# Two gate pairs in seven quarter products in every feed-forward of a two-layer trunk, and the S5 preparation moved behind them

## Chip, core and metric

One core of a Trainium2 chip runs the whole program in one launch. The metric is the device time of one execution in microseconds (us), as the median of the runs shown.

## What is computed

Two layers, each a gated feed-forward, a token mixer and another gated feed-forward, on 256 tokens of 1024 columns; a norm at the end. The feed-forward is what the change touches:

```python
def swiglu(h, wg, wu, wd):
    return (jax.nn.silu(h @ wg) * (h @ wu)) @ wd      # wg, wu: 1024 x 2816, wd: 2816 x 1024

for l in range(2):
    x = x + 0.5 * swiglu(rmsnorm(x, ffn1_norm[l]), ffn1_wg[l], ffn1_wu[l], ffn1_wd[l])   # "a0", "a1"
    x = x + hybrid_mixer(rmsnorm(x, mix_norm[l]), ...)   # an S5 branch and an mLSTM branch
    x = x + 0.5 * swiglu(rmsnorm(x, ffn2_norm[l]), ffn2_wg[l], ffn2_wu[l], ffn2_wd[l])   # "b0", "b1"
return rmsnorm(x, final_norm)
```

The S5 branch needs tables that come from its parameters alone (exponentials, sines, small complex products), so they can be made ahead of it.

## The kernel before

**Split products.** All operands are float32. Each is split into a high and a low part, and every product takes three matmuls (`mm3`, L281 to L283: high x high, high x low, low x high). A weight tile of 128 x 1024 is loaded by a DMA on SP's queue (L239), ACT casts it to the high part `wh` (L263), and DVE subtracts that for the low part `wl` (L264). Six such pairs fit (`W_SLOTS`), and four raw tiles.

**A feed-forward** (`ffn`) goes over the 2816 columns in blocks of 512: b = 0 to 4, and a half block b = 5. A block is a gate `unit` (wg), a Silu on ACT, an up `unit` (wu), and a multiply on DVE (L580) that gives the hidden values `sg`. One block later `turns` transposes them on PE (L513, into PSUM tiles `hT`), and they are split again: ACT casts `hh` (L331), DVE subtracts for `hl` (L332). Then `project` multiplies with wd over 22 chunks k and adds to x. PSUM has four `mm` tiles for these sums and four `aux` tiles, which `hT` and the three tiles `qx`, `qy`, `qz` of a pair share.

**A pair** (`pair`, `seven`) does the gate products of two neighbouring blocks at once. Tokens, the 1024 inputs and the 1024 columns are each cut in two, and seven products of quarters stand for eight, as in Strassen's method in Winograd's form. A product is 12 matmuls of 512 columns. The sums of x's quarters are made once per feed-forward by `combine` (four DVE operations, L415 to L418, and four splits into `sh`, `sl`). The quarters of the weights are eight tiles `r` of 128 x 1024 (two each of `r00`, `r10`, `r01`, `r11`, in ten slots, loaded by L445). Sums of weight quarters replace the tiles in place: two by accumulating DMAs on POOL's queue (L452, `r00 += w01` after product 1, `r01 += w11`), two by DVE (L454). Each product's two tiles are cast on ACT (L459) and subtracted on DVE (`wl`, L460). Between the products stand the chunks of the two up units (`steps`, eight of them; multiply at L545), and `turns` comes at the second of eight steps. The products run in the order 1, 2, 5, 6, 7, 4, 3; `qy` holds product 2 until DVE adds it to `q1` (L476), `qz` holds product 5 until L490. In names, `wl_51_b0g3` is the second tile of product 5 in the pair that begins at block 3 of `b0`.

Before, `PAIRS` names one pair in the feed-forwards b: blocks 1 and 2 of `b0` and `b1`. All other blocks are plain.

**The S5 preparation** (`s5_prep`) is a generator of 19 steps, given to the feed-forwards a as `bg`. The order of the code is a request: a scheduler arranges the instructions on each engine as tiles and slots allow. `next(bg, None)` runs one step at each half of a plain block and at each k of `project`; `pair` calls it nowhere. With no pair in a feed-forward a, 12 steps stand in the blocks and the rest in `project`.

Of the kernel before, what the change touches and what calls it, by code (L numbers as in the profile page):

```python
# [35 lines left out]
B_SLOTS = 10  # L36
T_SLOTS = 8
N_S = 64
PAIRS = {"b": (1,)}
RS_SCALE = -(0.5**13)  # L40
NPAIR = 16
NC2 = L // 2
# [105 lines left out]
class Trunk:  # L148
# [351 lines left out]
    def ffn(self, normed, wg, wu, wd, name, after, bg=iter(())):  # L500
        nc = self.nc
        xh, xl = normed.out
        hT = []

        def turn(b, n, h):
            m = n // P
            new = self.a4 if b else self.v4
            hp = new([P, 4, L], f"hh_{name}_{b}", F32R)
            lp = new([P, 4, L], f"hl_{name}_{b}", F32R)
            for t in range(NT):  # L510
                pt = self.aux(f"hT_{name}_{b}_{t}").rearrange("p (a n) -> p a n", a=4)
                for a in range(m):
                    nc.tensor.transpose(pt[:, a, :], h[t][:, a * P : (a + 1) * P], self.ident)  # L513
                s = slice(t * P, (t + 1) * P)
                self.split(hp[:, :m, s], lp[:, :m, s], pt[:, :m, :])
            hT.extend((hp[:, a, :], lp[:, a, :]) for a in range(m))

        todo = []

        def turns():  # L520
            for i in todo:
                turn(*i)
            todo.clear()

        def pair(b, c0):

            sg = {}
            gate = self.seven(wg, c0, (xh, xl), sums, f"{name}g{b}")
            ups = [self.steps(wu, c0 + 512 * j, 512, xh, xl, f"{name}u{b + j}") for j in range(2)]
            for i in range(8):  # L530
                done = next(gate, {})
                for (t, j), g in done.items():
                    s = g if (t, j) != (1, 0) else self.t2([P, 512], f"sg_{name}_{b}_{t}")
                    nc.scalar.activation(s, g, AF.Silu, scale=normed.rs[t])
                    sg[t, j] = s
                if i == 1:
                    turns()
                ua = next(ups[i // 4])
                if i in (5, 7):
                    j = i // 6  # L540
                    if j == 0:
                        ua = first
                    for t in range(NT):
                        s = sg[t, j]
                        nc.vector.scalar_tensor_tensor(s, ua[t], normed.rs[t], s, op0=ALU.mult, op1=ALU.mult)  # L545
                    todo.append((b + j, 512, [sg[t, j] for t in range(NT)]))
                if i == 3:
                    first = ua

        pairs = PAIRS.get(name[0], ())  # L550
        sums = None
        for b, c0 in enumerate(range(0, DFF, 512)):
            if b in pairs:
                pair(b, c0)
            if b in pairs or b - 1 in pairs:
                continue
            n = min(512, DFF - c0)
            cold = normed.rs[0] is None
            with ExitStack() as order:
                if cold:  # L560
                    order.enter_context(self.behind())
                    order.enter_context(normed.first(0))
                ga = self.unit(wg, c0, n, xh, xl, f"{name}g{b}", (lambda: normed.turn(1)) if b == 0 else None,
                               early=[self.b4] * 4 if b == 0 else [], back=1 if cold else 2)
            if cold:
                with normed.first():
                    normed.whole()
            turns()
            sg = []
            with normed.first() if b == 0 else nullcontext():  # L570
                for t in range(NT):
                    s = self.t2([P, 512], f"sg_{name}_{b}_{t}")[:, :n]
                    nc.scalar.activation(s, ga[t], AF.Silu, scale=normed.rs[t])
                    sg.append(s)
                next(bg, None)
                ua = self.unit(wu, c0, n, xh, xl, f"{name}u{b}")
            if b == 0 and pairs:
                sums = self.combine(normed.quads, name)
            for t in range(NT):
                nc.vector.scalar_tensor_tensor(sg[t], ua[t], normed.rs[t], sg[t], op0=ALU.mult, op1=ALU.mult)  # L580
            next(bg, None)
            todo.append((b, n, sg))
        turns()
        return self.project(hT, wd, 0.5, name, W_SLOTS, after, bg)
# [738 lines left out]
```

## Time and profile before

| | |
|---|---|
| runs | 1238.13, 1237.85, 1237.78 us; median 1237.85 |
| profiled execution | 1238.24 us, its span 1236.5 us |
| PE / DVE / ACT / POOL busy | 99% / 74% / 58% / 2% of the span |
| instructions on PE / DVE / ACT | 6875 / 1594 / 1046 |
| DMA | 226.33 MB, mean 183 GB/s |
| granted TensorE clock | 0.999 |

PE is the tensor engine, DVE the vector engine, ACT the scalar engine, POOL the engine whose queue carries the accumulating DMAs. Busy is the share of time in which an engine runs an instruction; matmuls overlap in the trace, so the distance from one start to the next (the pitch) tells what one costs. `x12` behind a row is the number of such instructions. A bracket behind a row is idle time of that engine just before it and what ended it. In the program, `a0` runs from about 20 to 199 us, and blocks 1 to 4 of `b0` from about 457 to 549 us.

### The profile page before, as it was taken

What the parts mean: (1) busy time and instruction counts of PE and PEld (TensorE: products, weight loads), DVE (VectorE), ACT (ScalarE), POOL (GpSimd) and SP (SyncE); (2) the same over time, 40 slices, a digit from 0 to 9 for tenths busy, and PEclk for the clock granted to TensorE, in tenths of its full rate; (3) what the DMA queues carried; (4) which work ended last, traced back from release to release, by engine and by line L of the source; (5) the groups of instructions that cost most, each with busy time, mean ns of one, the idle gap of its engine ahead of it and who ended that gap; (6) DMA issues with size and microseconds to landing.
All of it is one profiled execution on the core that took longest, in us unless ns stands there. A gap on an engine that the chain in (4) does not pass through costs nothing.

```text
span 1236.5 us, 18416 instructions
## 1 busy us (share of the span) xinstructions
PE 1223.4 (99%) x6875; PEld 1052.9 (85%) x6875; DVE 912.2 (74%) x1594; ACT 716.2 (58%) x1046; POOL 26.5 (2%) x58
## 2 busy tenths in 40 slices
PE   9999999999999999999999999999999999999997
PEld 7888888989898888888888888889898978888886
DVE  7865856898989789654577668478989887885544
ACT  6455644655986467453455556365568854764441
POOL 2000000000000010000000000000000000100000
PEclk9999999999999999999999999999999999999999
DMA  7775574675555676665656655646645555956561
GB/s 242 237 195 178 143 226 122 195 217 148 165 169 171 209 222 182 204 185 178 200 172 190 191 177 165 202 144 196 203 137 154 174 167 187 288 173 186 173 210 44
DMA packets 130122, 226.33 MB, mean 183 GB/s; under 512 B 18328, under 2 KB 57456, under 8 KB 130032
## 3 DMA queue, kind: packets, MB, share of 16 engines
q1 hardware_dynamic: 127440, 219.88, 57.9%
q0 software_dynamic: 2528, 5.25, 2.1%
q8 instruction: 54, 0.88, 0.3%
q14 instruction: 36, 0.29, 0.1%
q10 hardware_dynamic: 64, 0.02, 0.0%
HBM read 223.01 MB, written 1.06 MB: 181 GB/s over the span
## 4 chain that ended last, share of the span: by engine, by line
PE 94%; DVE 3%; issue 2%; ACT 1%; DMA 0%; DVEq 0%; ACTq 0%
PE dn_b L282 3%; PE dn_b L281 3%; PE dn_b L283 3%; PE dn_a L281 3%; PE dn_a L282 3%; PE dn_a L283 3%; PE acc_a1g L281 2%; PE acc_a0g L282 2%; PE acc_a1g L283 2%; PE acc_a0u L281 2%; PE acc_b0u L281 2%; PE acc_a1u L282 2%; PE acc_b1u L281 2%; PE acc_a1u L283 2%; PE acc_b1u L283 2%; PE acc_a0u L283 2%
## 5 line engine op out<-in xcount | busy, mean ns | idle before, releaser
L264 DVE TENSOR_TENSOR wl_b<-raw_b,wh_b 128x1024 fp32r<-128x1024 f32 x44 | 53.9, 1225 | 60.9 <-ACT wh_b L263 60.9
L263 ACT CAST wh_b<-raw_b 128x1024 fp32r<-128x1024 f32 x44 | 46.3, 1052 | 68.1 <-PE dn_b L283 51.4
L264 DVE TENSOR_TENSOR wl_a<-raw_a,wh_a 128x1024 fp32r<-128x1024 f32 x44 | 53.6, 1221 | 34.9 <-ACT wh_a L263 34.9
L263 ACT CAST wh_a<-raw_a 128x1024 fp32r<-128x1024 f32 x44 | 45.9, 1050 | 44.2 <-PE dn_a L283 27.7
L281 PE MATMUL dn_a<-wh_a,hh_a 128*128 128x512 f32 x176 | 69.2, 393 | 0.0
L281 PE MATMUL dn_b<-wh_b,hh_b 128*128 128x512 f32 x176 | 69.0, 392 | 0.0
L282 PE MATMUL dn_a<-wl_a,hh_a 128*128 128x512 f32 x176 | 68.8, 391 | 0.0
L282 PE MATMUL dn_b<-wl_b,hh_b 128*128 128x512 f32 x176 | 68.8, 391 | 0.0
L283 PE MATMUL dn_b<-wh_b,hl_b 128*128 128x512 f32 x176 | 68.7, 390 | 0.0
L283 PE MATMUL dn_a<-wh_a,hl_a 128*128 128x512 f32 x176 | 68.5, 389 | 0.0
L283 PE MATMUL acc_g<-wh_g,xl_m 128*128 128x412 f32 (+1 forms) x160 | 56.7, 354 | 0.2
L281 PE MATMUL acc_g<-wh_g,xh_m 128*128 128x412 f32 (+1 forms) x160 | 56.4, 352 | 0.0
L282 PE MATMUL acc_g<-wl_g,xh_m 128*128 128x412 f32 (+1 forms) x160 | 55.9, 350 | 0.0
L263 ACT CAST wh_g<-raw_g 128x824 fp32r<-128x824 f32 (+1 forms) x40 | 34.9, 882 | 31.2 <-PE acc_g L283 10.9
L264 DVE TENSOR_TENSOR wl_g<-raw_g,wh_g 128x824 fp32r<-128x824 f32 (+1 forms) x40 | 40.1, 1012 | 14.4 <-ACT wh_g L263 14.1
L281 PEld LDWEIGHTS dn_a<-wh_a,hh_a 128*128 128x128 f32 x176 | 33.0, 188 | 7.1
L281 PEld LDWEIGHTS dn_b<-wh_b,hh_b 128*128 128x128 f32 x176 | 33.0, 188 | 7.1
L283 PEld LDWEIGHTS dn_a<-wh_a,hl_a 128*128 128x128 f32 x176 | 33.1, 188 | 7.0
L283 PEld LDWEIGHTS dn_b<-wh_b,hl_b 128*128 128x128 f32 x176 | 33.1, 188 | 6.9
L282 PEld LDWEIGHTS dn_b<-wl_b,hh_b 128*128 128x128 f32 x176 | 33.1, 188 | 6.9
L282 PEld LDWEIGHTS dn_a<-wl_a,hh_a 128*128 128x128 f32 x176 | 33.1, 188 | 6.7
L264 DVE TENSOR_TENSOR wl_a1g<-raw_a1g,wh_a1g 128x1024 fp32r<-128x1024 f32 x22 | 26.8, 1222 | 15.9 <-ACT wh_a1g L263 15.8
(593 smaller groups left out, 4020.1 us busy)
## 6 DMA issues: line engine op xcount, KB each, us to landing
raw_a<-in_ffn_wd_dram SPq DMA_DIRECT2D x44, 512.0 KB, 3.8
raw_b<-in_ffn_wd_dram SPq DMA_DIRECT2D x44, 512.0 KB, 3.6
raw_g<-in_w_in_dram SPq DMA_DIRECT2D x32, 412.0 KB, 4.2
raw_a0u<-in_ffn_wu_dram SPq DMA_DIRECT2D x22, 512.0 KB, 5.1
raw_b0u<-in_ffn_wu_dram SPq DMA_DIRECT2D x22, 512.0 KB, 4.5
raw_a1g<-in_ffn_wg_dram SPq DMA_DIRECT2D x22, 512.0 KB, 3.7
raw_a1u<-in_ffn_wu_dram SPq DMA_DIRECT2D x22, 512.0 KB, 4.0
raw_b1u<-in_ffn_wu_dram SPq DMA_DIRECT2D x22, 512.0 KB, 4.8
```

The lines of the kernel that those rows point to most:

```text
L263: nc.scalar.copy(wh[:, d], r[:, d])
L264: nc.vector.tensor_tensor(wl[:, d], r[:, d], wh[:, d].bitcast(F32), op=ALU.subtract)
L281: mm(ps, xh, wh, start=start, stop=False, skip_group_check=more)
L282: mm(ps, xh, wl, start=False, stop=False, skip_group_check=more)
L283: self.pe = mm(ps, xl, wh, start=False, stop=stop, skip_group_check=more).ins
```

## The change

`PAIRS` gets a second pair (blocks 3 and 4) in `b0` and `b1`, and both pairs in `a0` and `a1`: eight pairs instead of two. `combine` moves behind the multiply of block 0. Since `pair` runs no step of `bg`, four plain half-block places are left for it in a feed-forward a; the other 15 steps run in `project`.

```diff
-PAIRS = {"b": (1,)}
+PAIRS = {"a": (1, 3), "b": (1, 3)}
...
                 next(bg, None)
                 ua = self.unit(wu, c0, n, xh, xl, f"{name}u{b}")
-            if b == 0 and pairs:
-                sums = self.combine(normed.quads, name)
             for t in range(NT):
                 nc.vector.scalar_tensor_tensor(sg[t], ua[t], normed.rs[t], sg[t], op0=ALU.mult, op1=ALU.mult)
             next(bg, None)
+            if b == 0 and pairs:
+                sums = self.combine(normed.quads, name)
             todo.append((b, n, sg))
```

Counted over the whole program, the change takes 72 matmuls of 128x512 from PE (24 each at L281, L282 and L283). DVE gets 84 subtractions at L460, 24 adds at L454, 18 of L476, L490 and L496, eight at L415 to L418 and eight more splits, and loses 48 at L264; ACT gets 84 casts at L459, 18 copies at L467 and eight splits and loses 48 casts at L263. POOL issues 32 accumulating DMAs instead of eight, SP as many loads as before. The multiplies of the paired blocks go from L580 to L545, and L580 is L578 afterwards.

**Place 1: PE in `b0`, where the hidden values of blocks 1 and 2 are transposed.** Before, in the plain block 3:

```order
L283 MATMUL acc_b0g3_1_5189<-wh_b0g3_6_0_5246,xl_b0_4600 128x512
L513 MATMUL hT_b0_1_0_5264<-ident_87,q1_b0g1_4866 128x128 x4
L513 MATMUL hT_b0_1_1_5271<-ident_87,sg_b0_1_1_5106 128x128 x4
L513 MATMUL hT_b0_2_0_5280<-ident_87,q6_b0g1_5018 128x128 x4
L513 MATMUL hT_b0_2_1_5287<-ident_87,q7_b0g1_5060 128x128 x4
L281 MATMUL acc_b0u3_0_5298<-wh_b0u3_0_0_5302,xh_b0_4599 128x512
L282 MATMUL acc_b0u3_0_5298<-wl_b0u3_0_0_5303,xh_b0_4599 128x512
```

And now, in the second pair:

```order
L282 MATMUL qy_b0g3_5256<-wl_21_b0g3_5319,xh_b0_4666 128x512
L283 MATMUL qy_b0g3_5256<-wh_21_b0g3_5318,xl_b0_4667 128x512
L513 MATMUL hT_b0_1_0_5332<-ident_87,q1_b0g1_4933 128x128 x4
L513 MATMUL hT_b0_1_1_5339<-ident_87,sg_b0_1_1_5173 128x128 x4
L281 MATMUL acc_b0u3_0_5284<-wh_b0u3_2_0_5364,xh_b0_4666 128x512
L513 MATMUL hT_b0_2_0_5348<-ident_87,q6_b0g1_5085 128x128 x4
L282 MATMUL acc_b0u3_0_5284<-wl_b0u3_2_0_5365,xh_b0_4666 128x512
L283 MATMUL acc_b0u3_0_5284<-wh_b0u3_2_0_5364,xl_b0_4667 128x512
...
L282 MATMUL acc_b0u3_1_5285<-wl_b0u3_2_0_5365,xh_b0_4666 128x512
L513 MATMUL hT_b0_2_1_5355<-ident_87,q7_b0g1_5127 128x128 x4
L283 MATMUL acc_b0u3_1_5285<-wh_b0u3_2_0_5364,xl_b0_4667 128x512
L281 MATMUL qz_b0g3_5257<-wh_50_b0g3_5386,sh0_b0_4889 128x512
```

The four transposes stood in a row, between two units. Now they follow product 2 (`qy`) one by one, with matmuls of the up unit between them, and product 5 (`qz`) comes behind. `hT_b0_2_0` is the third `aux` tile wanted while `qx`, `qy` and `qz` hold three of the four.

**Place 2: DVE around the same time.** Before:

```order
L264 TENSOR_TENSOR wl_b0g3_6_0_5247<-raw_b0g3_6_5244,wh_b0g3_6_0_5246 128x1024
L264 TENSOR_TENSOR wl_b0u3_0_0_5303<-raw_b0u3_0_5300,wh_b0u3_0_0_5302 128x1024
L545 SCALAR_TENSOR_TENSOR q6_b0g1_5018<-acc_b0u2_0_5064,z2_b0_0_4569,q6_b0g1_5018 128x512
L545 SCALAR_TENSOR_TENSOR q7_b0g1_5060<-acc_b0u2_1_5065,z2_b0_1_4648,q7_b0g1_5060 128x512
L264 TENSOR_TENSOR wl_b0u3_2_0_5321<-raw_b0u3_2_5318,wh_b0u3_2_0_5320 128x1024
L264 TENSOR_TENSOR wl_b0u3_4_0_5339<-raw_b0u3_4_5336,wh_b0u3_4_0_5338 128x1024
L264 TENSOR_TENSOR wl_b0u3_6_0_5357<-raw_b0u3_6_5354,wh_b0u3_6_0_5356 128x1024
L264 TENSOR_TENSOR wl_b0g4_0_0_5379<-raw_b0g4_0_5376,wh_b0g4_0_0_5378 128x1024
L332 TENSOR_TENSOR hl_b0_1_5263<-hT_b0_1_0_5264,hh_b0_1_5262 128x4x128
L332 TENSOR_TENSOR hl_b0_1_5263<-hT_b0_1_1_5271,hh_b0_1_5262 128x4x128
```

And now:

```order
L264 TENSOR_TENSOR wl_b0u3_2_0_5365<-raw_b0u3_2_5362,wh_b0u3_2_0_5364 128x1024
L460 TENSOR_TENSOR wl_50_b0g3_5387<-r000_b0g3_5258,wh_50_b0g3_5386 128x1024
L454 TENSOR_TENSOR r000_b0g3_5258<-r000_b0g3_5258,r110_b0g3_5424 128x1024
L460 TENSOR_TENSOR wl_51_b0g3_5397<-r001_b0g3_5260,wh_51_b0g3_5396 128x1024
L454 TENSOR_TENSOR r001_b0g3_5260<-r001_b0g3_5260,r111_b0g3_5426 128x1024
L264 TENSOR_TENSOR wl_b0u3_4_0_5409<-raw_b0u3_4_5406,wh_b0u3_4_0_5408 128x1024
L476 TENSOR_TENSOR q1_b0g3_5282<-q1_b0g3_5282,qy_b0g3_5256 128x512
L460 TENSOR_TENSOR wl_60_b0g3_5431<-r000_b0g3_5258,wh_60_b0g3_5430 128x1024
L460 TENSOR_TENSOR wl_61_b0g3_5441<-r001_b0g3_5260,wh_61_b0g3_5440 128x1024
L332 TENSOR_TENSOR hl_b0_1_5331<-hT_b0_1_0_5332,hh_b0_1_5330 128x4x128
L332 TENSOR_TENSOR hl_b0_1_5331<-hT_b0_1_1_5339,hh_b0_1_5330 128x4x128
L332 TENSOR_TENSOR hl_b0_2_5347<-hT_b0_2_0_5348,hh_b0_2_5346 128x4x128
```

The splits `hl` had one multiply pair and subtractions of plain weight tiles ahead of them. Now the subtractions of product 5 and two adds of weight quarters stand ahead of `q1`'s add (L476), which frees `qy`; the splits of block 1 come two subtractions later. The POOL queue has the second pair's accumulating DMAs in the order `r010`, `r011`, `r000`, `r001`; `wl_51` is made of `r001`.

**Place 3: DVE in `a0`, at the end of the half block 5.** Before:

```order
L264 TENSOR_TENSOR wl_a0_4_0_1598<-raw_a0_4_1595,wh_a0_4_0_1597 128x1024
L580 SCALAR_TENSOR_TENSOR sg_a0_5_0_1347<-acc_a0u5_0_1357,z2_a0_0_286,sg_a0_5_0_1347 128x256
L580 SCALAR_TENSOR_TENSOR sg_a0_5_1_1349<-acc_a0u5_1_1358,z2_a0_1_307,sg_a0_5_1_1349 128x256
L264 TENSOR_TENSOR wl_a0_5_0_1629<-raw_a0_5_1626,wh_a0_5_0_1628 128x1024
L332 TENSOR_TENSOR hl_a0_5_1442<-hT_a0_5_0_1443,hh_a0_5_1441 128x2x128
L332 TENSOR_TENSOR hl_a0_5_1442<-hT_a0_5_1_1448,hh_a0_5_1441 128x2x128
```

And now:

```order
L628 TENSOR_TENSOR bbo_s0_1478<-b_s0_1457,qre_s0_1446 128x256
L628 TENSOR_TENSOR bbw_s0_1479<-b_s0_1457,qim_s0_1447 128x256
L628 TENSOR_TENSOR bbo_s0_1478<-b_s0_1457,qre_s0_1446 128x256
L628 TENSOR_TENSOR bbw_s0_1479<-b_s0_1457,qim_s0_1447 128x256
L578 SCALAR_TENSOR_TENSOR sg_a0_5_0_1241<-acc_a0u5_0_1304,z2_a0_0_286,sg_a0_5_0_1241 128x256
L628 TENSOR_TENSOR bbo_s0_1478<-bbo_s0_1478,bbw_s0_1479 128x256 x2
L628 TENSOR_TENSOR abo_s0_1504<-bbo_s0_1478,are_s0_1398 128x256
L578 SCALAR_TENSOR_TENSOR sg_a0_5_1_1243<-acc_a0u5_1_1305,z2_a0_1_307,sg_a0_5_1_1243 128x256
L332 TENSOR_TENSOR hl_a0_5_1405<-hT_a0_5_0_1406,hh_a0_5_1404 128x2x128
L628 TENSOR_TENSOR abw_s0_1505<-bbo_s0_1478,aim_s0_1399 128x256
```

Seven small operations of the S5 preparation (L628, 128x256) now stand before and between the two multiplies of block 5 (L578), whose results PE transposes before `project` begins.

## Rows read from the trace of the kernel before

**Rows 1.** The page's first lines: the span, and busy time (share of the span) and instructions of each engine.

```profile
span 1236.5 us, 18416 instructions
PE 1223.4 (99%) x6875; PEld 1052.9 (85%) x6875; DVE 912.2 (74%) x1594; ACT 716.2 (58%) x1046; POOL 26.5 (2%) x58
```

**Rows 2.** The waits of PE in the whole program: who waited, for whom; us in total, times, longest. Under them, from the page, the engines' shares in the chain that ended last.

```profile
PE warm L207 <- POOL ident masks.py:199: 1.5, 1, 1.5
PE xT_m L92 <- DVE sq_m L78: 1.3, 2, 0.6
PE aT L1020 <- DVE al L1017: 0.8, 2, 0.4
PE gainsT L199 <- DMA gains<-in_ffn_norm_dram: 0.8, 1, 0.8
PE acc_a0g L282 <- DVE wl_a0g L264: 0.2, 1, 0.2
...
PE 94%; DVE 3%; issue 2%; ACT 1%; DMA 0%; DVEq 0%; ACTq 0%
```

**Rows 3.** The timeline of PE in `b0` (start, duration, line, operation): the first matmul of the first pair, the first of its product 7, the first of block 3's gate, and the transposes of blocks 1 and 2.

```profile
457.31 0.39 PE L281 MATMUL qx_b0g<-wh_b0g,xh_b 128*128 128x512 f32 x1
...
479.98 0.39 PE L281 MATMUL qx_b0g<-wh_b0g,sh_b 128*128 128x512 f32 x1
...
499.01 0.39 PE L281 MATMUL acc_b0g<-wh_b0g,xh_b 128*128 128x512 f32 x1
...
509.90 0.60 PE L513 MATMUL hT_b<-ident,q_b0g 128*128 128x128 f32 x4
510.33 0.60 PE L513 MATMUL hT_b<-ident,sg_b 128*128 128x128 f32 x4
510.77 1.04 PE L513 MATMUL hT_b<-ident,q_b0g 128*128 128x128 f32 x8
```

**Rows 4.** Busy time of each engine in stretches of the program (from:to in us, length, then busy us with instructions in brackets): `a0` from its start, its blocks, its `project`; the first pair of `b0`, and blocks 3 and 4 behind it. The last columns are clock, DMA share and GB/s.

```profile
20.00:32.00 12.00, 12.00 (x54) 9.69 (x52) 10.11 (x19) 8.67 (x12) 1.09 (x2) 1.00 0.68 217
32.00:141.00 109.00, 109.00 (x586) 92.89 (x586) 76.27 (x159) 58.80 (x86) 0.00 (x0) 1.00 0.68 199
141.00:199.00 58.00, 58.00 (x310) 47.81 (x309) 37.15 (x56) 30.10 (x48) 0.93 (x5) 1.00 0.55 166
456.00:502.00 46.00, 46.00 (x209) 38.19 (x208) 40.43 (x40) 29.33 (x33) 1.91 (x2) 1.00 0.75 212
502.00:549.00 47.00, 47.00 (x236) 39.87 (x235) 25.94 (x26) 22.99 (x27) 0.00 (x0) 1.00 0.61 181
```

**Rows 5.** DVE's and ACT's operations by form (count, busy us, mean ns of one, idle before).

```profile
L264 DVE TENSOR_TENSOR wl_b<-raw_b,wh_b 128x1024 fp32r<-128x1024 f32 x44 | 53.9, 1225 | 60.9 <-ACT wh_b L263 60.9
L460 DVE TENSOR_TENSOR wl_b0g<-r_b0g,wh_b0g 128x1024 fp32r<-128x1024 f32 x14 | 17.0, 1218 | 1.1 <-ACT wh_b0g L459 1.0
L332 DVE TENSOR_TENSOR sl_b<-s_b,sh_b 128x512 fp32r<-128x512 f32 x2 | 1.4, 686 | 0.0
L476 DVE TENSOR_TENSOR q_b0g<-q_b0g,qy_b0g 128x512 f32<-128x512 f32 x1 | 0.7, 680 | 0.0
L628 DVE TENSOR_TENSOR bbo_s<-b_s,qre_s 128x256 f32<-128x256 f32 x4 | 1.7, 421 | 2.4 <-DMA b_s<-in_s_b_re_dram 2.4
L603 DVE SCALAR_TENSOR_TENSOR eq_dt_s<-eq_dt_s,er_dt_s 128x16 f32<-128x16 f32 x12 | 2.1, 174 | 0.1
...
L459 ACT CAST wh_b0g<-r_b0g 128x1024 fp32r<-128x1024 f32 x14 | 14.7, 1052 | 5.3 <-DMA r_b0g<-in_ffn_wg_dram 1.6 <-issue 1.1 <-PE qx_b0g L283 0.9
```

**Rows 6.** The timeline of DVE in `b0`: `q1`'s add, the two subtractions of product 7, and the stretch in which block 3's first weight tiles are subtracted.

```profile
467.15 0.68 DVE L476 TENSOR_TENSOR q_b0g<-q_b0g,qy_b0g 128x512 f32<-128x512 f32 x1
...
473.49 2.35 DVE L460 TENSOR_TENSOR wl_b0g<-r_b0g,wh_b0g 128x1024 fp32r<-128x1024 f32 x2
...
489.25 0.74 DVE L545 SCALAR_TENSOR_TENSOR sg_b<-acc_b0u,z_b,sg_b 128x512 f32<-128x512 f32 x1
489.99 1.23 DVE L264 TENSOR_TENSOR wl_b0g<-raw_b0g,wh_b0g 128x1024 fp32r<-128x1024 f32 x1
492.18 2.59 DVE L264 TENSOR_TENSOR wl_b0g<-raw_b0g,wh_b0g 128x1024 fp32r<-128x1024 f32 x2 [0.97 <-ACT wh_b0g L263]
```

**Rows 7.** The accumulating DMAs: the issues in `b0` on POOL's queue, the summary of all eight of them, and ACT's cast that waited for the second.

```profile
449.24 1.25 POOL L452 DMA_DIRECT2D r_b0g<-in_ffn_wg_dram  x1 [111.87 <-DVE wl_b0g L460]
450.97 1.22 POOL L452 DMA_DIRECT2D r_b0g<-in_ffn_wg_dram  x1 [0.49 <-DVE wl_b0g L460]
453.08 1.19 POOL L452 DMA_DIRECT2D r_b0g<-in_ffn_wg_dram  x1 [0.89 <-DMA r_b0g<-in_ffn_wg_dram]
454.44 1.19 POOL L452 DMA_DIRECT2D r_b0g<-in_ffn_wg_dram  x1 [0.16 <-issue]
...
  ACT wh_b1g L459: 3.0, 2
  ACT wh_b0g L459: 1.6, 1
...
DMA to landing us min/median/max: 9.1/12.7/16.8
...
462.46 1.05 ACT L459 CAST wh_b0g<-r_b0g 128x1024 fp32r<-128x1024 f32 x1 [1.64 <-DMA r_b0g<-in_ffn_wg_dram]
```

## Prediction

> **What bounds the kernel now.** I read the page's first lines first. PE is busy 1223.4 of 1236.5 us [rows 1]. Busy PE is not yet PE at its peak, so the list of PE's waits comes next: in the whole program it waits about 4.6 us, 1.5 of them at the start, and the chain that ended last is 94% PE [rows 2]. The reader should see that almost nothing can be won by ending a wait, and that a matmul taken out shortens the program by its pitch, as long as PE's operands stay ahead of it. Then the stretches: DVE, which makes the low parts, is busy 40.43 of 46 us in the first pair of `b0` and 25.94 of 47 us in the plain blocks behind it; in `a0` it is busy 76.27 of 109 us in the blocks and 37.15 of 58 in `project` [rows 4]. PE is busy through all these stretches. So the question is whether DVE, and the accumulating DMAs that it waits for, keep up with seven products in places where they had eight plain ones.
>
> The profiled execution took 1238.24 us, 1.7 more than its span and 0.4 over the median of 1237.85. The sum is made against 1238.24.
>
> **The change, term by term.**
>
> *Matmuls removed.* From the first matmul of the pair in `b0` (457.31) to the first of block 3 (499.01) are 41.70 us [rows 3]: 7 products and 8 chunks of 12 matmuls, 180 in all, and two transposes, for which two of the later ones took 509.90 to 510.77, 0.87 us [rows 3]. That is (41.70 - 0.87) / 180 = 0.2268 us for a matmul. The change takes out 72, all on the path: **-16.3 us**. Nothing is added on PE.
>
> *Second pairs, four of them.* This is the first place where I expect something back. In `b0` call the start of the second pair T = 499.01. PE does three groups of 12 matmuls (8.16 us), the transposes of block 1 (0.87) and one matmul (0.23), and wants the third transpose tile at T + 9.26 = 508.3. That needs an `aux` tile, and it comes when DVE's add of `q1` frees `qy`. On DVE this add now stands behind `wl_51` and `wl_51` behind an accumulating DMA (place 2). When does that DMA land? The second pair's first two subtractions take the places of block 3's first two and end at 491.2 and 493.4 [rows 6]; then `r000` and `r001` may be issued. The quickest of the eight accumulating DMAs landed 9.1 us after its issue [rows 7]. In `b0` that is 449.24 + 9.1 = 458.3, and ACT's cast of the second tile began when it landed, at 462.46 [rows 7], so they follow at 4.1 us. That gives 500.3 for `r000` and 504.4 for `r001`. Behind it stand ACT's cast (1.05), `wl_51` (1.22), an add and an up tile (1.13 each, the pitch in the pair of rows that takes 2.35) and the add itself (0.68) [rows 5, 6]: 509.6. PE waits 1.3 us. A cross-check: in the first pair, where the same chain exists, `q1`'s add ended at 467.15 + 0.68 = 467.8 [rows 6], 10.5 us after the pair began, also 1.3 us past 9.26. There it did no harm, because only two transpose tiles were wanted. Behind it, `hT_b0_2_1` and `qz` wait for the splits of block 1, which follow two subtractions after the add: some 0.3 us more. So 1.6 us a pair, **+6.4 us** for four. After this DVE has room: it ended product 7's subtractions at 475.84, and PE began product 7 at 479.98 [rows 3, 6]. From below this term is 0, if the DMAs land earlier; from above it is 7.4 us a pair, if `r001` needs the longest time seen, 16.8 us [rows 7], instead of the 11.0 used. I take the value near the quick end, since by 491 the first two accumulating DMAs of the pair, whose tiles come free when product 7 is subtracted (475.84) and the add behind it is done, should have landed.
>
> *First pairs in `a0` and `a1`.* `combine` moves into the time of the pair: eight operations of 0.686 us [rows 5], 5.5 us, between product 2 and `q1`'s add. In `b` they stand before it. PE can feel this at product 5 and 6; the lead of 4.1 us at product 7 [rows 3, 6] bounds it at 1.4 us, and 0 is the other end. I take 0.5 each: **+1.0 us**.
>
> *End of block 5 in `a0` and `a1`.* Between the two multiplies stand three S5 operations now (place 3) where there were none. At a pitch of about 0.35 under their mean of 0.421 us [rows 5] the second transpose comes about 1.0 us after the first, which itself takes 0.43 [rows 3]: 0.6 each, **+1.2 us** (0, or 2.0 each if the four before the first multiply count too).
>
> *DVE as a whole.* A pair has 14 subtractions and 4 adds for 8 plain subtractions, 10 more of 1.22 us, and three small adds of 0.68: 14.2 us [rows 5]. In the second pair of `b0` that makes 25.94 + 14.2 = 40.1 of 47 - 2.7 = 44.3 us, 91%. The first pair had 40.43 of 46, 88%, without a wait of PE [rows 2, 4], so this passes. In `a0` the three stretches sum to 123.5 us of 179 [rows 4]; two pairs and `combine` add 33.9, and 24 matmuls less leave 173.6 us: 157.4, or 91% over the whole feed-forward. The steps moved to `project` make this even, but the order still lets about 50 small exponential operations (0.174 us each [rows 5]) into the second pair. I put 0.5 us each on it: **+1.0 us**. ACT gets six casts (1.05 us) and three copies no longer than that a pair, under 9.5 on 22.99 of 47 us [rows 4, 5]: no bound. SP issues as many loads as before. The DMA share was 0.75 with a pair and 0.61 to 0.68 in plain blocks [rows 4]: it goes up, and stays under one.
>
> Sum: -16.3 + 6.4 + 1.0 + 1.2 + 1.0 = -6.7 us, 1231.5 against the profiled time and **1231.2 us** against the median.
>
> **A rule weighed.** The quickest accumulating DMA of 512 KB took 9.1 us to landing and the median 12.7 [rows 7]. The Trainium skill ("DMA: Bandwidth & Descriptors", section "Anatomy of one DMA") fits a DMA issued by GpSimd as 2.0 us plus its bytes at 436 GB/s, an estimate of 3.2 us here, by which `r001` would have landed before the second pair began and the term of 6.4 us would be 0. The trace disagrees with it by a factor of three, so I go by the trace.
>
> **Rivals.**
>
> *No stall anywhere.* The DMAs of the second pair run in a quieter queue, or `aux` tiles come free another way. Then the time is 1238.2 - 16.3 = 1221.9 us. For it: the first pair shows no wait [rows 2]. Against it: the third `aux` tile, which the first pair does not want there. 0.15.
>
> *DVE becomes the bound in the feed-forwards a.* In the first pair of `b0` it was idle 12% of the time, waiting for ACT, PE or DMA. If it can't do with less, 157.4 us of work need 157.4 / 0.88 = 178.9 us, 5.3 more than PE's 173.6. Twice that is 10.6, and with the second pairs' 6.4 us the sum is +0.7: 1238.9 us, no difference. For it: 91% is more than any stretch of [rows 4] shows. Against it: in the first 12 us of `a0` DVE is busy 84% and PE stays full. 0.2, spread on both sides of no difference.
>
> *The accumulating DMAs land late, and it is slower.* One mechanism: in each second pair `r001` gates `wl_51`, this gates `q1`'s add, and this gates PE at the third transpose. It decides from a stall of 3.3 us a pair on, since then 4 x 3.3 + 3.2 equals 16.3; that is `r001` landing 12.7 us after its issue instead of 11.0, which is the median of those seen [rows 7]. At the 16.8 of the slowest the stall is 7.4 us and the time 1238.2 - 16.3 + 29.6 + 3.2 = 1254.7 us. For it: DMAs issued together queue at 4.1 us each, and a tile that comes free late pushes all behind it. Against it: here the four are issued in two groups some 10 us apart. 0.1. The Trainium skill ("SBUF — State Buffer", section "SBUF: two separate sides") has a mechanism on this side: DVE copies in a two-port mode keep GpSimd from writing the descriptors of its DMAs, so a busier DVE would delay them; no row here separates that from queueing.
>
> *The change does not do what it says*, in that the scheduler lets S5 steps into the pairs: the order shows it for the small operations alone, about 8.7 us of DVE, and that is in the last term.
>
> **How the numbers follow.** My forecast has 0.52, no stall 0.15, DVE as the bound 0.2, late DMAs 0.1, anything else 0.03. A measurement of this kernel can tell some 0.2% (2.5 us) from no change. Faster by more than that: forecast nearly whole, no stall, under half of the DVE case: 0.75. Within it: 0.12. Slower: late DMAs mostly and the worse part of the DVE case: 0.13. The likeliest case alone reaches from 1226 to 1236. The range goes to no stall at the low end and past the DVE case at the high end, and leaves the late DMAs out: 1221.5 to 1241.
>
> **What would show it.** Right: 6803 instructions on PE instead of 6875 [rows 1]; in each second pair a wait of PE of 1 to 2 us at the third `hT` tile, ended by DVE's L476; waits under 1 us at products 5 and 6 of the first pairs and at the last `hT` in the feed-forwards a; PE's waits in all about 14 us instead of 4.6; DVE about 1008 us busy, 96 more (six pairs at 14.2 and two `combine` at 5.5). Wrong: no wait at `hT` (no stall), waits of PE for `wl` tiles spread over `a0` and `a1` (DVE as the bound), or ACT's casts of `r` waiting several us for DMA in the second pairs (late DMAs).

## The result: 1% slower, not 0.5% faster

The changed kernel takes 1250.15 us (median of 4, 1248.03 to 1255.12) against 1237.94: a ratio of 1.0103, interval 1.0091 to 1.0115. The forecast was 1231.2 and its range ended at 1241.0. The profiled execution took 1248.96 us, its span 1247.3, 10.8 more than before. One execution of experiment 6 below took 1499.62 us at a mean granted clock of 0.753, and its numbers leave it out. First the page's lines that answer to [rows 1, 2]: the span, the busy times, and the chain that ended last by engine and, below, by line.

```profile
span 1247.3 us, 18542 instructions
PE 1219.1 (98%) x6803; PEld 1044.4 (84%) x6803; DVE 996.8 (80%) x1688; ACT 765.2 (61%) x1108; POOL 54.8 (4%) x82
PE 78%; DMA 8%; DVE 7%; issue 3%; ACT 2%; POOL 1%; SPq 0%; DVEq 0%; ACTq 0%; POOLq 0%
PE dn_b L282 3%; PE dn_b L281 3%; PE dn_b L283 3%; PE dn_a L281 3%; PE dn_a L282 3%; PE dn_a L283 3%; DMA r_b1g<-in_ffn_wg_dram 2%; DMA r_a0g<-in_ffn_wg_dram 2%; PE acc_b0u L282 1%; PE acc_b0u L283 1%; PE acc_b0u L281 1%; PE acc_g L283 1%; PE acc_a1u L282 1%; PE acc_a1u L283 1%; PE acc_a1u L281 1%
```

PE has 72 instructions less, as counted, and DVE is at 80%. But the chain was 94% PE [rows 2] and is 78% now, with 8% DMA, and the DMAs named are the loads and sums of weight quarters, `r_b1g` and `r_a0g`. PE's waits in the whole program (us in total, times, longest), which were 4.6 us in all [rows 2] and are 19.5 now; these six are new:

```profile
PE hT_a L513 <- DVE q_a0g L476: 4.4, 1, 4.4
PE hT_a L513 <- DVE q_a1g L476: 4.2, 1, 4.2
PE cols L645 <- DMA rows<-in_ml_skip_dram: 1.9, 1, 1.9
PE hT_a L513 <- DVE sg_a L578: 1.7, 2, 1.1
PE hT_b L513 <- DVE q_b0g L476: 1.6, 1, 1.6
...
PE hT_b L513 <- DVE q_b1g L476: 1.3, 1, 1.3
```

The waits foreseen at the third transpose tile are there, in `b` at the size foreseen (1.6 and 1.3 us) and in `a` at nearly three times it. The third row, a wait for parameter rows, is in no term of the prediction. By stretches, cut where PE begins the next feed-forward or mixer:

| stretch | before, us | after, us | change | 0.2268 x matmuls removed | given back |
|---|---|---|---|---|---|
| start and `a0` | 199.0 | 209.7 | +10.7 | -5.4 | 16.1 |
| mixer | 232.0 | 232.0 | 0 | 0 | 0 |
| `b0` | 184.6 | 183.9 | -0.7 | -2.7 | 2.0 |
| `a1` | 193.4 | 195.1 | +1.7 | -5.4 | 7.1 |
| mixer | 232.0 | 232.0 | 0 | 0 | 0 |
| `b1` | 195.5 | 194.6 | -0.9 | -2.7 | 1.8 |

So most of it, 23.2 of 27.0 us, is lost in `a0` and `a1`. The windows of `a0` (from:to, length, busy us with instructions for PE, PEld, DVE, ACT and POOL, granted clock, DMA share, GB/s) show how:

```profile
20.00:32.00 12.00, 12.00 (x55) 9.94 (x54) 9.99 (x19) 9.49 (x13) 3.71 (x3) 1.00 1.01 307
32.00:36.00 4.00, 2.06 (x9) 1.10 (x7) 3.06 (x5) 1.47 (x3) 1.20 (x1) 0.96 1.15 207
36.00:45.00 9.00, 9.00 (x22) 5.75 (x22) 4.65 (x9) 3.94 (x8) 0.00 (x0) 0.50 1.09 298
81.00:91.00 10.00, 10.00 (x50) 8.39 (x48) 6.18 (x12) 3.23 (x4) 0.00 (x0) 1.00 0.95 241
91.00:96.00 5.00, 0.60 (x4) 0.30 (x4) 4.56 (x6) 4.14 (x6) 0.00 (x0) 0.77 0.00 0
96.00:100.00 4.00, 4.00 (x15) 3.31 (x14) 3.73 (x5) 1.45 (x3) 0.00 (x0) 0.50 0.44 131
```

Twice PE stops, and its clock falls behind the stop. From 32 to 36 us it is busy for 2.06 us; from 36 to 45 the granted clock is 0.50, the lower of its two levels (1.2 GHz). From 91 to 96 it is busy for 0.60, and from 96 to 100 the clock is 0.50 again. The DMA share is at or near one ahead of each stop, and 0 in the second, since the last accumulating DMA had landed at 90.3. In `a1` there is only the stop at the third tile: behind its 4.2 us the clock is 0.57 from 708 to 712 us. The waits make 7.4 of `a0`'s 16.1 us (4.4, 1.9 and, at block 5, 1.1); the slow clock is most of the rest. The first stop on PE's timeline:

```profile
32.82 0.39 PE L282 MATMUL acc_a0u<-wl_a0u,xh_a 128*128 128x512 f32 x1
35.16 0.24 PE L645 MATMUL cols<-ident,rows 56*128 56x56 f32 x1 [1.95 <-DMA rows<-in_ml_skip_dram]
...
38.36 0.63 PE L281 MATMUL qx_a0g<-wh_a0g,xh_a 128*128 128x512 f32 x1
38.78 0.63 PE L282 MATMUL qx_a0g<-wl_a0g,xh_a 128*128 128x512 f32 x1
39.21 0.63 PE L283 MATMUL qx_a0g<-wh_a0g,xl_a 128*128 128x512 f32 x1
```

PE stands before a transpose of the S5 step's parameter rows (L645), whose small loads were issued behind the pair's first loads and landed 10.2 us after their issue (5.0 before). Then a matmul takes 0.43 us instead of 0.2268. The 24 instructions from 35.32 to 45.73 take 10.4 us; in experiment 6 the same 24 take 6.2, so the clock costs 4.2 us here. The second stop starts on POOL's queue in `a0`:

```profile
68.73 1.19 POOL L452 DMA_DIRECT2D r_a0g<-in_ffn_wg_dram  x1 [33.42 <-ACT wh_a0g L459]
70.11 1.20 POOL L452 DMA_DIRECT2D r_a0g<-in_ffn_wg_dram  x1 [0.19 <-issue]
75.26 1.19 POOL L452 DMA_DIRECT2D r_a0g<-in_ffn_wg_dram  x1 [2.09 <-DVE wl_a0g L460]
76.60 1.20 POOL L452 DMA_DIRECT2D r_a0g<-in_ffn_wg_dram  x1 [0.15 <-issue]
...
86.56 1.05 ACT L459 CAST wh_a0g<-r_a0g 128x1024 fp32r<-128x1024 f32 x1 [3.37 <-DMA r_a0g<-in_ffn_wg_dram]
90.36 1.05 ACT L459 CAST wh_a0g<-r_a0g 128x1024 fp32r<-128x1024 f32 x1 [2.26 <-DMA r_a0g<-in_ffn_wg_dram]
...
91.44 1.23 DVE L460 TENSOR_TENSOR wl_a0g<-r_a0g,wh_a0g 128x1024 fp32r<-128x1024 f32 x1 [1.31 <-ACT wh_a0g L459]
94.98 0.68 DVE L476 TENSOR_TENSOR q_a0g<-q_a0g,qy_a0g 128x512 f32<-128x512 f32 x1
...
95.72 1.11 PE L513 MATMUL hT_a<-ident,q_a0g 128*128 128x128 f32 x4 [4.40 <-DVE q_a0g L476]
```

The four sums of the second pair are issued at 68.7 to 76.6; these answer to [rows 7]. ACT's casts of `r000` and `r001` wait until 86.56 and 90.36 for their landing, 11.2 and 13.7 us after the issue. Then `wl_51`, an add, an up tile, `q1`'s add, and at 95.72 PE's transpose, 4.40 us late.

### The profile page after: what moved, and what is told of

Its sections match the earlier page's. It is cut to its first block, busy times and chain, and to the rows that moved or that the text cites. A ratio compares the mean times of both kernels' runs of the same rounds, so it can differ in the third digit from the quotient of the medians.

```text
span 1247.3 us, 18542 instructions
## 1 busy us (share of the span) xinstructions
PE 1219.1 (98%) x6803; PEld 1044.4 (84%) x6803; DVE 996.8 (80%) x1688; ACT 765.2 (61%) x1108; POOL 54.8 (4%) x82
## 4 chain that ended last, share of the span: by engine, by line
PE 78%; DMA 8%; DVE 7%; issue 3%; ACT 2%; POOL 1%; SPq 0%; DVEq 0%; ACTq 0%; POOLq 0%
PE dn_b L282 3%; PE dn_b L281 3%; PE dn_b L283 3%; PE dn_a L281 3%; PE dn_a L282 3%; PE dn_a L283 3%; DMA r_b1g<-in_ffn_wg_dram 2%; DMA r_a0g<-in_ffn_wg_dram 2%; PE acc_b0u L282 1%; PE acc_b0u L283 1%; PE acc_b0u L281 1%; PE acc_g L283 1%; PE acc_a1u L282 1%; PE acc_a1u L283 1%; PE acc_a1u L281 1%
## 5 line engine op out<-in xcount | busy, mean ns | idle before, releaser
L264 DVE TENSOR_TENSOR wl_b<-raw_b,wh_b 128x1024 fp32r<-128x1024 f32 x44 | 53.9, 1226 | 58.5 <-ACT wh_b L263 58.5
L263 ACT CAST wh_b<-raw_b 128x1024 fp32r<-128x1024 f32 x44 | 46.3, 1053 | 63.8 <-PE dn_b L283 50.5
L264 DVE TENSOR_TENSOR wl_a<-raw_a,wh_a 128x1024 fp32r<-128x1024 f32 x44 | 53.4, 1221 | 23.4 <-ACT wh_a L263 23.4
L281 PE MATMUL dn_a<-wh_a,hh_a 128*128 128x512 f32 x176 | 70.2, 399 | 0.0
L282 PE MATMUL dn_a<-wl_a,hh_a 128*128 128x512 f32 x176 | 69.1, 393 | 0.0
L281 PE MATMUL dn_b<-wh_b,hh_b 128*128 128x512 f32 x176 | 68.9, 392 | 0.0
L282 PE MATMUL dn_b<-wl_b,hh_b 128*128 128x512 f32 x176 | 68.8, 391 | 0.0
L283 PE MATMUL dn_a<-wh_a,hl_a 128*128 128x512 f32 x176 | 68.7, 390 | 0.0
L283 PE MATMUL dn_b<-wh_b,hl_b 128*128 128x512 f32 x176 | 68.7, 390 | 0.0
L263 ACT CAST wh_a<-raw_a 128x1024 fp32r<-128x1024 f32 x44 | 45.8, 1049 | 28.2 <-PE dn_a L283 17.3
L283 PE MATMUL acc_g<-wh_g,xl_m 128*128 128x412 f32 (+1 forms) x160 | 56.7, 354 | 0.2
L281 PE MATMUL acc_g<-wh_g,xh_m 128*128 128x412 f32 (+1 forms) x160 | 56.4, 352 | 0.0
L282 PE MATMUL acc_g<-wl_g,xh_m 128*128 128x412 f32 (+1 forms) x160 | 56.0, 350 | 0.0
L263 ACT CAST wh_g<-raw_g 128x824 fp32r<-128x824 f32 (+1 forms) x40 | 34.8, 883 | 30.7 <-PE acc_g L283 13.1
L264 DVE TENSOR_TENSOR wl_g<-raw_g,wh_g 128x824 fp32r<-128x824 f32 (+1 forms) x40 | 40.1, 1013 | 13.8 <-ACT wh_g L263 13.6
L460 DVE TENSOR_TENSOR wl_a0g<-r_a0g,wh_a0g 128x1024 fp32r<-128x1024 f32 x28 | 33.8, 1221 | 10.5 <-ACT wh_a0g L459 10.4
L459 ACT CAST wh_a0g<-r_a0g 128x1024 fp32r<-128x1024 f32 x28 | 29.2, 1051 | 17.8 <-DMA r_a0g<-in_ffn_wg_dram 5.6
L459 ACT CAST wh_a1g<-r_a1g 128x1024 fp32r<-128x1024 f32 x28 | 29.2, 1053 | 17.6 <-DMA r_a1g<-in_ffn_wg_dram 5.4
L460 DVE TENSOR_TENSOR wl_a1g<-r_a1g,wh_a1g 128x1024 fp32r<-128x1024 f32 x28 | 33.6, 1221 | 7.1 <-ACT wh_a1g L459 6.8
L283 PEld LDWEIGHTS dn_a<-wh_a,hl_a 128*128 128x128 f32 x176 | 33.1, 188 | 7.1
L281 PEld LDWEIGHTS dn_b<-wh_b,hh_b 128*128 128x128 f32 x176 | 33.0, 188 | 7.1
L281 PEld LDWEIGHTS dn_a<-wh_a,hh_a 128*128 128x128 f32 x176 | 33.0, 188 | 6.9
```

The costliest lines, as they stand in the source:

```text
L263: nc.scalar.copy(wh[:, d], r[:, d])
L264: nc.vector.tensor_tensor(wl[:, d], r[:, d], wh[:, d].bitcast(F32), op=ALU.subtract)
L281: mm(ps, xh, wh, start=start, stop=False, skip_group_check=more)
L282: mm(ps, xh, wl, start=False, stop=False, skip_group_check=more)
L283: self.pe = mm(ps, xl, wh, start=False, stop=stop, skip_group_check=more).ins
L459: nc.scalar.copy(wh, t)
```

## Experiments

Each is a change of the changed kernel unless it says otherwise, with its median and its ratio to the kernel before. My theory after the result was of three separate costs: the wait at the third tile, a0's wait for the rows, and block 5. The rival was DVE without slack.

**1. Pairs in `b` alone** (`PAIRS = {"b": (1, 3)}`).

> Second pairs in the feed-forwards b alone (24 matmuls less than before; a plain). Theory (three separate costs: the wait of the third transpose tile for q1's add behind the accumulating DMAs in every second pair, 4.4 and 4.2 us in a, 1.6 and 1.3 in b; a wait for the S5 rows in a0 with half clock behind it, 7.3; the order at block 5, 1.7): -5.4 + 1.9 + 1.5 = -2.0, 1235.9 us. Rival (DVE at 91% is the bound wherever pairs stand): no gain, 1238 or more.

1236.92 us against 1238.33, 0.9991 (0.9981 to 1.0000). PE's waits at `hT` were 2.2 and 1.4 us, and the clock stayed at 1.00 behind the longer one (506 to 526 us). The change is close to no use even where it does no harm: 5.4 us less work, 3.6 of them waited away.

**2. One pair in each, the late one in `a`** (`PAIRS = {"a": (3,), "b": (1,)}`).

> One pair in each feed-forward, blocks 3 and 4 in a, blocks 1 and 2 in b (24 matmuls less than before). Theory: behind a plain block only two transpose tiles are wanted in the pair, and the pair's loads come long after the start, so neither the wait at the third tile nor the one for the rows is there: -5.4 and up to 1.7 back at block 5, 1232.5 to 1234.2 us. Rival (DVE bound): the same DVE work of a pair stands beside more S5 steps, so 1237 to 1240 with waits of PE for weight tiles.

1245.73, 1.0061 (1.0039 to 1.0083): a miss of over 10 us, for the theory. PE waited 3.8 and 3.1 us for `q1`'s add with no third tile wanted, at product 5. A row of DVE's waits, and below it how long `b_s` took to land:

```profile
DVE bbo_s L628 <- DMA b_s<-in_s_b_re_dram: 11.4, 2, 8.4
...
DMA to landing us min/median/max: 13.4/13.7/14.0
```

An S5 operation stood on DVE in front of the pair's and waited up to 8.4 us for its own load `b_s`, which took 13.4 to 14.0 us to land where it had taken 6.2 in the kernel before. In `a0` DVE then ran without a stop from 86.0 us up to `q1`'s add at 94.4. So it was not the third tile as such. What these waits share with the rows' is a load behind the pair's DMAs.

**3. Transposes one step later, 4. one step earlier.**

```diff
-                if i == 1:
+                if i == (2 if b == 3 else 1):   # 3: turn2b
+                if i == (0 if b == 3 else 1):   # 4: turn0
                     turns()
```

> The whole change, with the transposes of the second pairs asked for one step later, behind product 5, when q1's add has freed qy. Theory: the four waits at the third tile (11.5 us) and the half clock behind two of them (3.1) go: 1235.5 us; the first wait that could take their place is product 5's second tile in a, which is ready 1 us ahead of PE. Rival (DVE bound): the lateness only moves to the next product, 1245 to 1250.

> The whole change, with the transposes of the second pairs asked for one step earlier, behind product 1, when qy and qz are not yet in use; DVE's order still has the splits of the first transposes behind wl_50, thus behind the landing of r000, but not behind q1's add. Theory: in b r000 lands early enough and the wait is gone (3 us in all); in a the wait stays at 3 to 4 us, now for hl (L332) at the fourth tile: 1246 to 1249. Rival (the aux tiles are the cause by their number alone): waits gone everywhere, 1235 to 1238.

Later gave 1247.49, 1.0078 (1.0061 to 1.0095), 12 us above the theory. The wait had moved: two rows of PE's waits.

```profile
PE hT_a L513 <- DVE hl_a L332: 8.9, 2, 4.5
PE hT_b L513 <- DVE hl_b L332: 2.9, 2, 2.2
```

With 2.0 us left at `q1`'s add, PE's waits at `hT` came to 13.8 us for 11.5 before this edit. PE now waited for the splits, which on DVE stand behind the same `wl_51` and, in `a0`, behind four more subtractions of weight quarters. What DVE did for PE after that operation was late, so moving PE's first need of it only moved the wait. The time lies in the rival's range, and that the lateness moves on was the rival's sign; whether DVE is the bound is left to experiment 6. Earlier gave 1243.09, 1.0048 (1.0022 to 1.0073), 3 us below the theory: in `b` the wait was gone (0.6 us in both), in `a` PE waited 5.7 us for `hl` (1.9 and 3.8), with the rows' 2.0 still there. So in `a` the number of `aux` tiles alone was not the cause.

**5. The S5 steps of a0's block 0 left to block 5 and `project`** (`cold` holds in that block only).

```diff
-                next(bg, None)
+                if not cold:
+                    next(bg, None)
...
-            next(bg, None)
+            if not cold:
+                next(bg, None)
```

> The whole change, with the two S5 steps of a0's block 0 left to block 5 and project, so that the loads of the rows do not follow the pair's first loads. Theory: the wait for the rows (2.1 us) and the half clock behind it (5.2) go: 1242.8 us. Rival (the half clock comes of something else, or DVE is the bound): 1249 to 1251, or more since project has two steps more.

1248.28, 1.0083 (1.0068 to 1.0098). The wait for the rows and the half clock at 36 us were gone (1.00 from 36 to 45), but by the medians only 1.9 of the 7.3 us expected were won, and the executions of the two kernels overlap: in `project` PE waited 3.0 us for the S5 tile `bs` (ACT L758, behind DVE's small operations), with a clock of 0.83 from 160 to 170 us. Taken out of one place, the steps were waited for in another.

**6. The sum `r00` on DVE, 7. the sum `r01` on DVE.**

```diff
-        add((0, 0), (0, 1), True)
+        add((0, 0), (0, 1))             # 6: dve_r00
-        add((0, 1), (1, 1), True)
+        add((0, 1), (1, 1))             # 7: dve_r01
```

> The whole change, with r00 += w01 as two DVE adds of loaded tiles instead of two accumulating DMAs (16 DMAs less, 16 adds of 1.2 us more in the program; r01 += w11 stays a DMA). Theory (the wait at the third transpose tile comes from the landing of r001 behind the other three accumulating DMAs): product 5's subtractions wait for no DMA, the waits of 4.4, 4.2, 2.1 and 1.5 us at hT shrink to under 1 each and the half clock behind them goes: 1236 to 1239 us. Rival (DVE has no slack, the landing only shows what was late anyway): DVE gets 2.3 us more a pair, the same waits or longer, 1250 to 1258.

> The whole change, with the other sum, r01 += w11, as two DVE adds instead of two accumulating DMAs; r00 += w01 stays a DMA, now with none ahead of it. Theory (the DMAs queue at 4 us each): in a0 r000 and r001 land about 9 us after their issue at 75.3 and 76.6, so near 84.4 and 88.4 instead of 86.5 and 90.3: the waits at hT in a fall by about 2 us each, those in b stay: 1244 to 1246. Rival (DVE bound): longer than 1250.

`r00` on DVE gave **1227.80 us, 0.9916 (0.9899 to 0.9932)**: 22 us less than the change, with 14.5 us more work on DVE (1011.3 busy), and 8 below the theory's range, which had left the wait for the rows standing. Its page line, the two longest of PE's waits that the kernel before did not have, and three of the windows shown above:

```profile
PE 1211.1 (99%) x6803; PEld 1039.2 (85%) x6803; DVE 1011.3 (82%) x1704; ACT 762.8 (62%) x1108; POOL 35.7 (3%) x66
...
PE hT_a L513 <- DVE sg_a L578: 1.2, 2, 0.7
PE dn_a L282 <- DVE wl_a L264: 0.8, 1, 0.8
...
36.00:45.00 9.00, 9.00 (x44) 6.98 (x43) 8.88 (x15) 7.57 (x13) 1.19 (x1) 1.00 1.09 277
81.00:91.00 10.00, 10.00 (x54) 8.42 (x53) 10.00 (x13) 7.94 (x11) 0.78 (x1) 1.00 0.84 203
91.00:96.00 5.00, 5.00 (x24) 4.14 (x23) 5.00 (x6) 2.19 (x4) 0.00 (x0) 1.00 0.35 105
```

DVE is busy for the whole 10 us from 81 to 91, where it had 6.18 in the changed kernel (the program is some us further on here), and PE stops nowhere. The clock is 1.00, and PE does 44 instructions from 36 to 45 instead of 22. So DVE had room, and idled for the DMAs. The wait for the rows is gone too: they landed in 8.3 us, with no accumulating DMA issued before 32 us (POOL did nothing from 20 to 32). The edit also moves the DMAs that are left: DVE now reads `r01` for the sum `r00`, and POOL's DMAs into `r01` wait for that add (L454).

`r01` on DVE took the same work to DVE and the same 8.4 MB from the DMAs, and gave 1242.08, 1.0033 (1.0023 to 1.0044), 2 us below the theory. In `a0` `r001` landed 9.7 us after its issue instead of 13.7, as DMAs that queue would have it; the waits at `hT` in `a` fell to 3.6 and 1.4 us, and 1.4 for the rows stayed. It matters which sums are DMAs, not only how many: `r00`'s sum can't be issued before product 1 is split and is wanted at product 5; `r01`'s is wanted at product 7 and, in the changed kernel, can go as soon as its tile is loaded.

**8. `r00` on DVE in the second pairs alone.**

```diff
-        add((0, 0), (0, 1), True)
+        add((0, 0), (0, 1), not name.endswith("g3"))
```

> The whole change, with r00's sum on DVE in the four second pairs alone; the first pairs keep their accumulating DMAs. Theory: the waits at hT in the second pairs (12.1 us) and the half clock behind them (3.4) go, a0's wait for the rows and its half clock (7.3 us in the profiled run, different from run to run) stay: 1234 to 1237 us, and with 1227.8 for all pairs this splits the loss into about two thirds at the second pairs and one third at a0's start. Rival (a0's start only cost so much because of what came later): 1227 to 1230.

1234.09, 0.9964 (0.9951 to 0.9977). So by the medians the sums of `r00` in the second pairs cost 16.1 us (1250.15 to 1234.09) and those in the first pairs 6.3 (to 1227.80). The eight executions lie from 1230.27 to 1236.78, those of the changed kernel from 1248.03 to 1255.12, so each share is good to a few us. In its trace PE still waited 1.0 us for the rows, and the clock from 36 to 45 us was 0.62.

**9. Experiment 2 with `r00` on DVE.**

> One pair in each feed-forward (a: blocks 3 and 4, b: blocks 1 and 2), with r00's sum on DVE. With the accumulating DMAs the same pairs gave 1245.7 us and qz waited 3.8 and 3.1 us for q1's add. Theory (landing of r000 and r001): the waits and the half clock behind them go, 1232.5 to 1235 us. Rival (there DVE came late to the pair by itself, since three plain blocks with S5 steps precede it): waits stay, 1243 to 1248.

1236.63, 0.9988 (0.9978 to 0.9997). The waits at product 5 fell from 3.8 and 3.1 to 0.5 each, `b_s` landed in 6.5 to 10.0 us. The rival, lateness of DVE's own, does not fit. But the time is 1.6 above the theory's upper end, and no run here says why.

**10. The kernel before with `r00` on DVE.**

> The kernel before with r00's sum on DVE in its two pairs. Theory: PE waited for nothing there, so nothing changes: 1237.5 to 1238.5 us. Rival (the DVE sum is better by itself, not through the wait): 1234 to 1236.

1238.17 against 1238.06, 1.0001 (0.9992 to 1.0011): where PE waited for nothing, replacing these DMAs wins nothing.

**11. Experiments 4 and 6 together, 12. the same and `r01` on DVE too.**

> Both: transposes behind product 1 and r00's sum on DVE. Theory: no wait at the transposes of second pairs nor at product 5; what is left is a0's wait for the rows with its half clock (7 us) and block 5 (1.7): 1234 to 1237 us. Rival (DVE bound): 1245 or more, with waits of PE for weight tiles.

> Transposes behind product 1, and all sums of weight quarters on DVE: no accumulating DMA left, four adds of 1.2 us more a pair than the change. Theory: the r01 DMAs were hidden already and only DVE gets longer: 1226 to 1229 us, no better than with r01 on a DMA (1226.7). Rival (the DMAs cost something wherever they run): 1222 to 1225. Rival (DVE bound at 83% busy plus 20 us): 1232 or more.

Together: **1226.71, 0.9906 (0.9890 to 0.9923)**, the best here, below the range expected, which had again left the wait for the rows standing; it is gone in this trace too. With `r01` too: 1231.71, 0.9948 (0.9933 to 0.9962), 5.0 us worse, above the theory's range and just under the 1232 of the DVE rival. PE now stood 2.4 us ahead of S5 products (`btp_s`, with no releaser shown), 1.8 at block 5 and 0.8 for a cast. With DVE 84% busy its slack seems to end here; that is argued from these waits, not isolated.

## Why the prediction failed, step by step

Two steps failed. The landing time of `r001` was taken from `b0` for all four second pairs, so their waits were 11.5 us and not 6.4. And two costs had no term: the slow clock behind a stop of PE, some 7.8 us, and PE's wait for the S5 rows, 2.0.

*Matmuls removed, -16.3.* Right: 6803 instructions on PE.

*Second pairs, +6.4.* The chain was the right one and in `b` its size too (1.6 and 1.3 us for 1.6). In `a` it was 4.4 and 4.2, so the four waits were 11.5 us: **this term was mis-sized.** Its landing time was worked out in `b0` and carried to `a0` and `a1`. The DMAs of `b0` in the changed kernel, and ACT's cast of `r001`:

```profile
493.26 1.18 POOL L452 DMA_DIRECT2D r_b0g<-in_ffn_wg_dram  x1 [28.03 <-DMA r_b0g<-in_ffn_wg_dram]
496.68 1.19 POOL L452 DMA_DIRECT2D r_b0g<-in_ffn_wg_dram  x1 [2.23 <-DVE wl_b0g L460]
502.14 1.18 POOL L452 DMA_DIRECT2D r_b0g<-in_ffn_wg_dram  x1 [4.28 <-DVE wl_b0g L460]
504.33 1.20 POOL L452 DMA_DIRECT2D r_b0g<-in_ffn_wg_dram  x1 [1.00 <-DVE wl_b0g L460]
...
515.36 1.05 ACT L459 CAST wh_b0g<-r_b0g 128x1024 fp32r<-128x1024 f32 x1 [2.22 <-DMA r_b0g<-in_ffn_wg_dram]
```

Those of `r010` and `r000` went out 9 us apart, and `r001` landed 11.0 us after its issue, as predicted. In `a0` it was 68.7 and 75.3, 6.5 us apart, and the DMAs, at about 4 us each, still queued: `r001` took 13.7 us, and 13.5 in `a1`. With these two numbers the prediction's own chain gives waits of 4.3 and 4.1. The rival of late DMAs put its turning point at 12.7 us. That rival, with 0.1, is in mechanism what happened, in two of the four pairs. One detail of place 1 was off: `qz` has no tile yet when the third transpose is wanted; `qx`, `qy` and the two transposes of block 1 hold the four.

With 11.5 us in place of 6.4 the sum would be 1236.6 us against the profiled time, still faster and inside the range. What made the kernel slower stood in the sum at nothing:

*What a wait costs.* **No term had it**: behind the 4.40 us stop the clock was at its lower level for about 4 us (15 instructions where experiment 6 had 20), behind the stop for the rows for about 9 (22 for 44). I priced waits by their own length. From the pitches I estimate 4.2 us behind the rows and 3.6 behind the two stops in `a` at the third tile. In `b` the clock stayed at 1.00 behind the stops (517 to 533 us in `b0`).

*First pairs in `a`, +1.0.* Wrong in kind: `combine` cost no wait, but the S5 rows' loads behind the pair's DMAs cost 2 us and, with the clock, some 6 in `a0`; experiment 8 has 6.3 for it. It differs from run to run: in the trace of experiment 3, which changes nothing there, this wait was 0.3 us and the clock stayed at 1.00. I had followed SP's order for the pair's tiles only, and passed by the small loads behind them, though the change puts more DMA into that stretch: a share of 0.68 [rows 4] became 1.01. The plain loads of the pair are in this too: without an accumulating DMA ahead of them (experiment 6) the rows still took 8.3 us for 5.0.

*End of block 5, +1.2.* Right in kind: 1.7.

*DVE as a whole, +1.0.* Right that it is no bound, and better than I thought: experiment 6 gave it more to do and was faster. The rival of DVE as the bound is refuted for the change; experiment 12 may show where it begins.

*The sum again, for the profiled execution:* -16.3 + 11.5 + 3.6 + 2.0 + 4.2 + 1.7 = +6.7 us, of +10.8 measured. The second pairs have 15.1 us of it, waits and clock together, where experiment 8 has 16.1. The 4.1 us left over are not placed; experiment 6, without these waits, has nearly as much (3.7, below).

*The rules weighed.* The estimate of 3.2 us by the Trainium skill ("DMA: Bandwidth & Descriptors", section "Anatomy of one DMA") missed again: the quickest of the 32 took 5.8, the median 10.4. Whether a busier DVE delays the descriptors, the prediction's other rule from the Trainium skill ("SBUF — State Buffer", section "SBUF: two separate sides"), was not isolated. The operations that the change adds on DVE are nearly all TENSOR_TENSORs of two tiles, not the copies of that rule; and in experiment 6, with DVE busier, the 16 DMAs of `r01` landed in 7.5 us in the median (10.4 is the median of both sums' DMAs). Both speak against it as the main cause.

Open: why experiment 9 keeps 1.6 us over its range, and the split of the 5.9 us by which experiment 6 stays short of 16.3 (1.2 at block 5, 1.0 for weight tiles in `project`; the rest, 3.7, is in no wait that these rows name).

## What to carry to other kernels

A DMA that does arithmetic in place can cost more than the same sum on a busy engine: look for the first operation in an engine's order that waits for it, and count as late what stands behind that operation, here `q1`'s add and PE's transposes. When a pattern that fits in one place is put in others, work out its landing times in each place anew, small loads on the same queues included. And price a stop of PE by more than its length: here the slow stretches behind three stops cost an estimated 7.8 us, against 16.3 of work saved.

## What the runs showed of the hardware

Accumulating DMAs of 512 KB that were issued close together landed about 4 us apart (the casts of `r000` and `r001` began 3.8 us apart in `a0`, 4.0 in `b0`), and the time from issue to landing ran from 5.8 to 17.8 us. Plain loads among them landed later too: the rows took 10.2 us, 8.3 with the pair's plain loads alone ahead of them (experiment 6), and 5.0 in the kernel before; `b_s` took up to 14.0 with `r00`'s accumulating DMAs (experiment 2), up to 10.0 without (experiment 9), and 6.2 in the kernel before.

The granted clock behind stops of PE: at the start of `a0` 0.50 for 9 us behind a stop of 1.95 us, 0.62 over the same stretch behind 1.0 us (experiment 8), 1.00 behind 0.3 us (experiment 3); in the second pair of `a0` 0.50 for 4 us behind 4.40 us; in `b0` 1.00 behind 1.65 us, and behind 2.17 us in experiment 1. So a longer stop did not have the longer slow stretch, and some stops had none.
